# The opening of a hybrid decoder trunk: modulation sums moved from VectorE to TensorE's column groups, and six product tiles instead of four

## The chip, the cores and the metric

One core of a Trainium2 chip runs the whole kernel in one launch. The metric is the device time of one execution in microseconds, the median of the runs shown. A profile is one execution recorded by the hardware profiler.

## The reference

Two layers; each is a SwiGLU feed-forward half-step, a mixing step (windowed attention, an RWKV-7 recurrence and a short convolution side by side) and a second SwiGLU half-step. Every sub-layer begins with an RMS norm whose result is scaled and shifted by columns that come from the conditioning vector `c`. The part around the change, cut to what matters:

```python
c_act = jax.nn.silu(c)                                   # (1, 1024)
for l in range(2):
    mod = (c_act @ w_ada[l] + b_ada[l]).reshape(1, 9, 1024)
    sh1, sc1, gt1, sh2, sc2, gt2, sh3, sc3, gt3 = ...     # nine rows of 1024
    hn = rms_norm(h, g_ffn1[l]) * (1.0 + sc1) + sh1       # h: (512 tokens, 1024)
    h = h + 0.5 * (1.0 + gt1) * swiglu(hn, w_ffn1_in[l], w_ffn1_out[l])
    ...                                                   # mixing and second SwiGLU, in the same manner
def swiglu(x, w_in, w_out):
    gate, up = jnp.split(x @ w_in, 2, axis=-1)            # 1024 -> 2 x 2816
    return (jax.nn.silu(gate) * up) @ w_out
```

## The kernel before

The residual lies transposed in SBUF: eight tiles `h[k]` of 128 features by 512 tokens (`T`, `KD` = 8). A float32 product is made of three TensorE matmuls in the format fp32r: both operands are split into a rounded part H and the rest L, and `mm3` adds wH·xH, wH·xL and wL·xH. A weight tile is split by `split`: ScalarE writes H, then VectorE writes L = source - H. One output tile (128 x 512) takes 8 x 3 = 24 matmuls of 512 columns and fills one bank of PSUM. PSUM has eight banks in four tags of two (`mm`, `r0`, `r1`, `x`).

The tile framework puts the instructions of each engine in a fixed order when the kernel is built, by the order of the program, its priorities and a model of when each is ready; `tc.issue_after(x)` and `tc.add_manual_dep` pin an instruction behind another on the same engine. Each engine then runs its list in order. SP issues the weight loads (`nc.sync.dma_start`), POOL (`nc.gpsimd.dma_start`) those of the later modulation weights.

`begin` (L1143 to L1255) is the opening. It makes the modulation of the first norm (rows sc1 and sh1 of layer 0, each 8 blocks of 128 columns) and the first four output tiles of the first SwiGLU's input product. Its modulation weights come in four groups `m` of two blocks each, in tiles of 1 MB. `scales(m)` and `shifts(m)` compute three of a group's four columns with `ada_dot` (L190), one VectorE instruction over 1024 elements that multiplies by a replicated silu(c) (`crep`, made by TensorE and ScalarE at L1200 to L1205) and sums along the row; the fourth column is made of eight TensorE matmuls with one moving column (L1180). `normed(k)` then makes block k of the normed activations: z = h·rstd on VectorE, reading rstd from PSUM; scale and shift on ScalarE (L1187); H on ScalarE, L on VectorE. `warm(n)` issues n matmuls whose result nobody reads. The groups of products go over n (output tile) and k (block): after the second product of group m, the modulation and norm of group m+1 are placed.

The pool `first` (L1257) holds the opening's modulation weights, raw weight tiles and small columns. When `begin` returns, the pool is closed and `ffn` (L337) opens its own pool in its place. `ffn` receives the finished PSUM tiles as `first`; `projector` (L292) goes on from there with the weights of tile 4 and later, up to tile 15, each loaded by SP into `wraw` (two buffers) and split into `wH` and `wL` (four buffers each in the pool `wp`). At the same time `ada_crep` (L194) loads c again into the new pool and `ada_steps` (L200) lets POOL load the next modulation columns, three buffers at a time, and VectorE sum them, in steps of 0, 0, 4, 4, 0, 3, 0, 0 behind the pairs of output tiles. After tile 15, `pair_in` makes the rest of the input product in another form (seven half-size products a pair).

Of the kernel before, what the change touches and what calls it, by code (L numbers as in the profile page):

```python
# [8 lines left out]
F32 = mybir.dt.float32  # L9
# [23 lines left out]
GAP = 448  # L33
GROUPS = ((0, 12), (12, 22))
# [24 lines left out]
def trunk_kernel(ctx, tc, ins, out, layers=L, phases=("ffn1", "mix", "ffn2")):  # L59
# [57 lines left out]
    def mm3(acc, w, k, x, sl, start, stop):  # L117
# [5 lines left out]
        mm(acc, wL, xH, start=False, stop=stop)  # L123
# [1019 lines left out]
    def begin(pool):  # L1143
# [3 lines left out]
        col = {n: pool.tile([P, KD], F32, name=n, tag=n) for n in ("sc", "sh", "gb", "gm0", "sh0")}  # L1147
        stt(col["gb"], bsc, 1.0, g1, ALU.add, ALU.mult)
        wa, wf, ws = {}, [], []

        def fetch(m):
            for n in (0, 2):
                w = pool.tile([P, 2, D], F32, name="wada", tag="wada", bufs=8)
                nc.sync.dma_start(w, ins["wa0"][m, :, n : n + 2])
                wa[m, n], wa[m, n + 1] = w[:, 0], w[:, 1]

        def fetch_w():
            j, g = divmod(len(wf), 2)
            w = pool.tile([P, KD, P], F32, name="wfirst", tag="wfirst", bufs=4)
            nc.sync.dma_start(w, ins["w1i"][0, j, g])  # L1160
            wf.append(w)

        def split_w(n):
            pair = tuple(wp.tile([P, KD, P], F32R, name=x, tag=x, bufs=4) for x in ("wH", "wL"))
            split(*pair, wf[n])
            ws.append(pair)

        def scales(m):
            for n in range(2):
                k = slice(2 * m + n, 2 * m + n + 1)  # L1170
                ada_dot(col["sc"][:, k], wa[m, n], crep)
                stt(col["gm0"][:, k], col["sc"][:, k], g1[:, k], col["gb"][:, k], ALU.mult, ALU.add)

        def shifts(m):
            k0, k1 = (slice(2 * m + n, 2 * m + n + 1) for n in range(2))
            ada_dot(col["sh"][:, k0], wa[m, 2], crep)
            tt(col["sh0"][:, k0], col["sh"][:, k0], bsh[:, k0], ALU.add)
            pt = psum([P, 1], "ps_ada")
            for k in range(KD):
                mm(pt, wa[m, 3][:, k * P : (k + 1) * P], cact[:, k : k + 1], start=k == 0, stop=k == KD - 1)  # L1180
            tt(col["sh0"][:, k1], pt, bsh[:, k1], ALU.add)

        def normed(k):
            z = E("z")
            tt(z, h[k], rstd, ALU.mult)
            x = E("hn_t")
# [184 lines left out]
```

## Time and profile before

| | |
|---|---|
| time, median of 3 runs | 1867.47 us (1863.78 to 1871.30) |
| profiled execution | 1866.04 us, span 1864.0 us |
| granted TensorE clock over the span | 0.994 |
| busy: PE, DVE, ACT, POOL | 1828.7, 1398.4, 836.3, 130.9 us |
| TensorE idle before the first product of the opening, and within it | 2.87 us, 1.56 us |
| read from HBM, mean rate | 302.66 MB, 164 GB/s |

Times in the rows are microseconds from the start of the span. PE is TensorE's matmul, PEld its weight load, DVE VectorE, ACT ScalarE, POOL GpSimd, SP the engine that issues DMAs. A timeline row has start, duration, engine, line, operation, output<-inputs, tile shape, count, and in brackets the engine's idle time before it and what ended that. A row of the groups has busy time, mean ns of one, idle time before and what ended it. Matmuls overlap in the pipeline: their spacing is read from start to start. An fp32 matmul shows as two instructions, an fp32r one as one.

### The profile page before, as it was taken

Reading aid. Unit: us, or ns where it says so; the run is one execution under the profiler, and the core shown is the slowest. Engines: PE = TensorE matmul, PEld = TensorE weight load, DVE = VectorE, ACT = ScalarE, POOL = GpSimd, SP = SyncE. Lnnn points to the kernel's source line nnn. Section 1 sums busy time; section 2 is a strip of 40 time slices with the busy share of each in tenths; the row PEclk is TensorE's granted clock in tenths of the full one; section 3 lists DMA queues with packets and bytes.
Section 4 is the critical chain, followed back from the end, with each engine's and each line's share of the span. In section 5 each row is a group of like instructions: output and inputs, shape, how many; then the busy total and the mean of one; then the engine's idle time right before and its main releaser. Section 6 shows DMA issues by size and latency. Waiting matters only on the chain.

```text
span 1864.0 us, 33421 instructions
## 1 busy us (share of the span) xinstructions
PE 1828.7 (98%) x13664; PEld 1644.4 (88%) x13664; DVE 1398.4 (75%) x2202; ACT 836.3 (45%) x1272; POOL 130.9 (7%) x212
## 2 busy tenths in 40 slices
PE   8999999999999999999999999999999999999999
PEld 6889899986777999899999988999767788998998
DVE  7687677867986887777878786777589778874872
ACT  4443255346422555245345524544563335532551
POOL 0101110100000000110100020110000000100100
PEclk8999999999999999999999999999999999999999
DMA  7667876621122475886737688773212125775752
GB/s 307 225 185 234 263 197 202 221 83 46 58 55 72 136 195 176 296 223 195 246 112 197 171 272 228 192 229 114 101 56 59 53 68 161 209 227 139 203 144 68
DMA packets 104313, 308.24 MB, mean 165 GB/s; under 512 B 23392, under 2 KB 24416, under 8 KB 103136
## 3 DMA queue, kind: packets, MB, share of 16 engines
q1 hardware_dynamic: 75936, 203.34, 32.3%
q0 software_dynamic: 28224, 102.77, 21.7%
q8 instruction: 107, 1.75, 0.4%
q14 instruction: 46, 0.38, 0.1%
HBM read 302.66 MB, written 3.41 MB: 164 GB/s over the span
## 4 chain that ended last, share of the span: by engine, by line
PE 71%; DVE 13%; DMA 7%; issue 4%; ACT 4%; POOL 1%; SPq 0%; POOLq 0%; DVEq 0%; ACTq 0%
PE ps_mm L121 11%; PE ps_mm L122 10%; PE ps_mm L123 10%; PE ps_d L420 6%; PE ps_d L422 6%; PE ps_d L421 6%; PE ps_f L420 3%; PE ps_f L422 3%; PE ps_f L421 3%; DMA wada<-in_wadaT 2%; DVE wL L135 2%; PE ps_g L422 2%; PE ps_g L420 2%; PE ps_g L421 2%; ACT wH L133 1%
## 5 line engine op out<-in xcount | busy, mean ns | idle before, releaser
L133 ACT CAST wH<-wraw 128x1024 fp32r<-128x1024 f32 (+2 forms) x292 | 266.1, 918 | 434.7 <-PE ps_mm L122 190.2
L135 DVE TENSOR_TENSOR wL<-wraw,wH 128x1024 fp32r<-128x1024 f32 (+2 forms) x292 | 307.2, 1058 | 105.1 <-ACT wH L133 104.4
L123 PE MATMUL ps_mm<-actH,wL 128*128 128x512 f32 (+1 forms) x784 | 281.5, 359 | 2.8 <-DVE wL L135 2.8
L121 PE MATMUL ps_mm<-actH,wH 128*128 128x512 f32 (+1 forms) x784 | 281.6, 359 | 0.0
L122 PE MATMUL ps_mm<-actL,wH 128*128 128x512 f32 (+1 forms) x784 | 281.2, 359 | 0.0
L121 PE MATMUL ps_mm<-hnH,wH 128*128 128x512 f32 (+1 forms) x760 | 267.5, 359 | 5.7 <-ACT hnH L133 2.9
L122 PE MATMUL ps_mm<-hnL,wH 128*128 128x512 f32 (+1 forms) x760 | 266.5, 353 | 0.5
L123 PE MATMUL ps_mm<-hnH,wL 128*128 128x512 f32 (+1 forms) x760 | 266.4, 353 | 0.6 <-DVE wL L135 0.6
L420 PE MATMUL ps_d<-comH,wH 128*128 128x256 f32 x816 | 224.7, 275 | 0.3 <-ACT s L446 0.3
L421 PE MATMUL ps_d<-comL,wH 128*128 128x256 f32 x816 | 224.4, 275 | 0.0
L422 PE MATMUL ps_d<-comH,wL 128*128 128x256 f32 x816 | 224.4, 275 | 0.0
L192 DVE SCALAR_TENSOR_TENSOR wada<-wada,crep 128x1024 f32<-128x1024 f32 x140 | 167.7, 1219 | 48.8 <-DMA wada<-in_wadaT 48.2
L135 DVE TENSOR_TENSOR wL<-sum,wH 128x1024 fp32r<-128x1024 f32 x102 | 124.9, 1224 | 71.5 <-ACT wH L133 71.3
L123 PEld LDWEIGHTS ps_mm<-actH,wL 128*128 128x128 f32 x784 | 149.1, 190 | 20.3 <-DVE wL L135 3.6
L121 PEld LDWEIGHTS ps_mm<-hnH,wH 128*128 128x128 f32 x760 | 143.4, 191 | 24.9 <-issue 3.8
L121 PEld LDWEIGHTS ps_mm<-actH,wH 128*128 128x128 f32 x784 | 149.1, 190 | 16.8
L122 PEld LDWEIGHTS ps_mm<-actL,wH 128*128 128x128 f32 x784 | 149.0, 190 | 16.8
L123 PEld LDWEIGHTS ps_mm<-hnH,wL 128*128 128x128 f32 x760 | 145.5, 191 | 19.3 <-issue 4.3
L122 PEld LDWEIGHTS ps_mm<-hnL,wH 128*128 128x128 f32 x760 | 145.4, 192 | 17.2 <-DVE hnL L277 1.6
L420 PEld LDWEIGHTS ps_d<-comH,wH 128*128 128x128 f32 x816 | 156.7, 192 | 0.9 <-ACT s L446 0.9
L422 PEld LDWEIGHTS ps_d<-comH,wL 128*128 128x128 f32 x816 | 156.7, 192 | 0.0
L421 PEld LDWEIGHTS ps_d<-comL,wH 128*128 128x128 f32 x816 | 156.7, 192 | 0.0
(354 smaller groups left out, 3855.6 us busy)
## 6 DMA issues: line engine op xcount, KB each, us to landing
wada<-in_wadaT POOLq DMA_DIRECT2D x128, 512.0 KB, 4.8
wraw<-in_wmi SPq DMA_DIRECT2D x40, 512.0 KB
wraw<-in_w2p SPq DMA_DIRECT2D x36, 512.0 KB
wraw<-in_w1p SPq DMA_DIRECT2D x32, 512.0 KB
wraw<-in_w1o SPq DMA_DIRECT2D x32, 384.0 KB
wraw<-in_w2o SPq DMA_DIRECT2D x32, 384.0 KB
wraw<-in_w1i SPq DMA_DIRECT2D x20, 512.0 KB
wraw<-in_w1o SPq DMA_DIRECT2D x32, 320.0 KB
```

What stands on the lines that cost most here:

```text
L121: mm(acc, wH, xH, start=start, stop=False)
L122: mm(acc, wH, xL, start=False, stop=False)
L123: mm(acc, wL, xH, start=False, stop=stop)
L133: nc.scalar.copy(hi, src)
L135: return nc.vector.tensor_sub(lo, src, hi.bitcast(F32))
L192: stt(w, w, 1.0, crep, ALU.mult, ALU.mult, accum_out=out_)
L420: mm(acc, wH, xH, start=start and i + k == 0, stop=False, skip_group_check=True)
L421: mm(acc, wH, xL, start=False, stop=False, skip_group_check=True)
L422: mm(acc, wL, xH, start=False, stop=k == 3, skip_group_check=True)
```

## The change

- The modulation weights of one block k, its scale and shift columns side by side (1024 rows by 256 columns, 1 MB), are one tile. `modulation(k)` streams them through TensorE: the stationary operand is a 32-column tile of `cz` whose first column is silu(c) and whose others are zero; the eight 128-row slices go in turn to four column groups of 32, so that four partial rows stand in PSUM. ScalarE copies the 128 x 256 result to `part`, two small matmuls with ones sum it into a scale column and a shift column, and VectorE makes `gm0` and `sh0` from them. The eight matmuls have high priority and are pinned behind each other and behind the product given as `behind`.
- `crep`, `scales` and `shifts` are gone from the opening.
- `normed` writes z = h·gm0·rstd in one VectorE instruction, with rstd copied to SBUF, H directly on ScalarE from z and the shift, L in one VectorE instruction; one ScalarE pass less for each block.
- Six output tiles are begun in the opening, not four. `begin` writes out the order of products, modulations, norms and weight splits by hand. Weights 4 and 5 are split into buffers of the pool `first`.
- The loads follow the list `WANTED`, one modulation tile and one weight tile in turn at first.
- A ScalarE instruction with Sqrt stands ahead of the squares. `warm` stands at other places, and its bank is of tag `x`.

```diff
--- before.py
+++ after.py
@@ -31,6 +31,7 @@
 BASE = 16
 PAD = 24
 GAP = 448
+WANTED = (0, 1, 0, 1, 0, 1, 0, 1, 0, 0, 1, 0, 1, 0)
 GROUPS = ((0, 12), (12, 22))
 RWKV_WORK, ATT_WORK, FILL_WORK = 29.8, 15.2, 129.6
 
@@ -120,7 +121,7 @@
         acc = paired(acc)
         mm(acc, wH, xH, start=start, stop=False)
         mm(acc, wH, xL, start=False, stop=False)
-        mm(acc, wL, xH, start=False, stop=stop)
+        return mm(acc, wL, xH, start=False, stop=stop)
 
     latest = {}
 
@@ -1144,114 +1145,131 @@
         hn = [tuple(hnp[k // 4].tile([P, T], F32R, name=n, tag="hn") for n in ("hnH", "hnL")) for k in range(KD)]
         g1 = prm(0, "g1")
         bsh, bsc = (prm(0, "b_ada")[:, i * KD : (i + 1) * KD] for i in range(2))
-        col = {n: pool.tile([P, KD], F32, name=n, tag=n) for n in ("sc", "sh", "gb", "gm0", "sh0")}
-        stt(col["gb"], bsc, 1.0, g1, ALU.add, ALU.mult)
-        wa, wf, ws = {}, [], []
-
-        def fetch(m):
-            for n in (0, 2):
-                w = pool.tile([P, 2, D], F32, name="wada", tag="wada", bufs=8)
-                nc.sync.dma_start(w, ins["wa0"][m, :, n : n + 2])
-                wa[m, n], wa[m, n + 1] = w[:, 0], w[:, 1]
+        col = {n: pool.tile([P, KD], F32, name=n, tag=n) for n in ("gb", "gm0", "sh0")}
+        wa, wf, ws = [], [], []
+
+        def fetch():
+            w = pool.tile([P, KD, 2 * P], F32, name="wada", tag="wada", bufs=6)
+            nc.sync.dma_start(w, ins["wa0"][len(wa)])
+            wa.append(w)
 
         def fetch_w():
             j, g = divmod(len(wf), 2)
-            w = pool.tile([P, KD, P], F32, name="wfirst", tag="wfirst", bufs=4)
+            w = pool.tile([P, KD, P], F32, name="wfirst", tag="wfirst", bufs=6)
             nc.sync.dma_start(w, ins["w1i"][0, j, g])
             wf.append(w)
 
         def split_w(n):
-            pair = tuple(wp.tile([P, KD, P], F32R, name=x, tag=x, bufs=4) for x in ("wH", "wL"))
-            split(*pair, wf[n])
+            home, bufs = (wp, 4) if n < 4 else (pool, 2)
+            pair = tuple(home.tile([P, KD, P], F32R, name=x, tag=x, bufs=bufs) for x in ("wH", "wL"))
+            split(*pair, wf[n], ("part", "row") if n else None)
             ws.append(pair)
 
-        def scales(m):
-            for n in range(2):
-                k = slice(2 * m + n, 2 * m + n + 1)
-                ada_dot(col["sc"][:, k], wa[m, n], crep)
-                stt(col["gm0"][:, k], col["sc"][:, k], g1[:, k], col["gb"][:, k], ALU.mult, ALU.add)
-
-        def shifts(m):
-            k0, k1 = (slice(2 * m + n, 2 * m + n + 1) for n in range(2))
-            ada_dot(col["sh"][:, k0], wa[m, 2], crep)
-            tt(col["sh0"][:, k0], col["sh"][:, k0], bsh[:, k0], ALU.add)
-            pt = psum([P, 1], "ps_ada")
-            for k in range(KD):
-                mm(pt, wa[m, 3][:, k * P : (k + 1) * P], cact[:, k : k + 1], start=k == 0, stop=k == KD - 1)
-            tt(col["sh0"][:, k1], pt, bsh[:, k1], ALU.add)
-
-        def normed(k):
-            z = E("z")
-            tt(z, h[k], rstd, ALU.mult)
-            x = E("hn_t")
-            act(x, z, AF.Identity, bias=col["sh0"][:, k : k + 1], scale=col["gm0"][:, k : k + 1])
-            split(*hn[k], x)
-
-        pw = psum([P, T], "ps_warm", "r1")
+        pw = psum([P, T], "ps_warm")
         wide = ones_r.unsqueeze(1).to_broadcast([P, 4, P])
 
-        def warm(n):
-
-            for _ in range(n):
-                mm(pw.rearrange("p (a b) -> p a b", b=P), ones_r, wide, start=True, stop=True)
+        def warm(n, behind=None):
+
+            with tc.issue_after(behind.ins) if behind else nullcontext():
+                for _ in range(n):
+                    mm(pw.rearrange("p (a b) -> p a b", b=P), ones_r, wide, start=True, stop=True)
 
         warm(3)
-
-        crep = pool.tile([P, D], F32, name="crep", tag="crep")
-        for hf in range(2):
-            pt = psum([P, 4, P], "ps_crep")
-            for k in range(4):
-                mm(pt[:, k], cT[:, 4 * hf + k : 4 * hf + k + 1].to_broadcast([P, P]), cst("ident"), start=True, stop=True)
-            act(crep[:, hf * 512 : hf * 512 + 512], pt.rearrange("p k n -> p (k n)"), AF.Silu)
-        fetch(0)
-        fetch_w()
-        fetch_w()
-        fetch(1)
-        fetch_w()
-        fetch_w()
-        fetch(2)
-        fetch(3)
+        cz = pool.tile([P, KD, CH // 2], F32, name="cz", tag="cz")
+        nc.gpsimd.memset(cz, 0.0)
+        nc.vector.tensor_copy(cz[:, :, 0], cact)
+        act(col["sh0"][:, :1], cact[:, :1], AF.Sqrt, bias=vals["eps"], scale=0.0)
+        for w in WANTED:
+            (fetch, fetch_w)[w]()
         nc.sync.dma_start(con[:, P:], ins["con"][:, P:])
-        warm(20)
+        warm(22)
+        stt(col["gb"], bsc, 1.0, g1, ALU.add, ALU.mult)
         ss = new_ss()
         for i in range(KD):
             add_ss(ss, i)
-
         pt = psum([P, NB], "ps_ss")
         for b in range(NB):
-            mm(pt[:, b : b + 1], ss[:, b * P : (b + 1) * P], ones[:, :1], start=True, stop=True)
-        warm(3)
+            m = mm(pt[:, b : b + 1], ss[:, b * P : (b + 1) * P], ones[:, :1], start=True, stop=True)
+        warm(3, m)
         r = pool.tile([P, NB], F32, name="rstd_t", tag="rstd_t")
         act(r, pt, AF.Sqrt, bias=vals["eps"], scale=1.0 / D)
         nc.vector.reciprocal(r, r)
-        rstd = psum([P, T], "ps_rstd", "r0")
+        pt = psum([P, T], "ps_rstd")
         for b in range(NB):
-            mm(rstd[:, b * P : (b + 1) * P], r[:, b : b + 1].to_broadcast([P, P]), cst("ident"), start=True, stop=True)
-        warm(2)
-        scales(0)
-        shifts(0)
-        warm(8)
+            mm(pt[:, b * P : (b + 1) * P], r[:, b : b + 1].to_broadcast([P, P]), cst("ident"), start=True, stop=True)
+        rstd = pool.tile([P, T], F32, name="rstd", tag="rstd")
+        nc.scalar.copy(rstd, pt)
+
+        def modulation(k, rest=0, behind=None):
+
+            pt = psum([P, 2 * P], "ps_ada")
+            with tc.high_priority():
+                for i in range(KD):
+                    j = slice(i % 4 * 32, i % 4 * 32 + 32)
+                    m = mm(pt[j], cz[:, i], wa[k][:, i], start=i < 4, stop=i >= 4)
+                    if behind is not None:
+                        tc.add_manual_dep(m.ins, behind.ins.name, ORDER, reason="column groups run together")
+                    behind = m
+            part = pool.tile([P, 2 * P], F32, name="part", tag="part", bufs=2)
+            latest["part"] = nc.scalar.copy(part, pt)
+            ada = m
+            warm(rest // 2, m)
+            pt = psum([P, 2], "ps_col")
+            for i in range(2):
+                last = mm(pt[:, i : i + 1], part[:, i * P : (i + 1) * P], ones[:, :1], start=True, stop=True)
+            warm(rest, last if rest else None)
+            c = slice(k, k + 1)
+            stt(col["gm0"][:, c], pt[:, :1], g1[:, c], col["gb"][:, c], ALU.mult, ALU.add)
+            tt(col["sh0"][:, c], pt[:, 1:], bsh[:, c], ALU.add)
+            return ada
+
+        def normed(k):
+            z, sh = E("hn_t"), col["sh0"][:, k : k + 1]
+            latest["row"] = stt(z, h[k], col["gm0"][:, k : k + 1], rstd, ALU.mult, ALU.mult)
+            act(hn[k][0], z, AF.Identity, bias=sh)
+            stt(hn[k][1], z, sh, hn[k][0].bitcast(F32), ALU.add, ALU.subtract)
+
+        pts = [psum([P, T], "ps_mm", tag) for tag in ("r0", "r1", "mm") * 2]
+
+        def go(*jobs):
+            for n, k in jobs:
+                last = mm3(pts[n], ws[n], k, hn[k], ALL, k == 0, k == KD - 1)
+            return last
+
+        split_w(0)
+        modulation(0, 4)
+        second = modulation(1)
         normed(0)
-        split_w(0)
+        with tc.issue_after(second.ins):
+            last = go((0, 0))
+        normed(1)
         split_w(1)
-        normed(1)
-        pts = [psum([P, T], "ps_mm", tag) for tag in ("mm", "mm", "r1", "r0")]
-        for m in range(4):
-            groups = [(n, 2 * m + k) for k in range(2) for n in range(4)]
-            if m == 0:
-                groups = [(n, k) for n0 in (0, 2) for k in range(2) for n in (n0, n0 + 1)]
-            elif m == 3:
-                groups = [(n, 6 + k) for n in range(4) for k in range(2)]
-            for g, (n, k) in enumerate(groups):
-                mm3(pts[n], ws[n], k, hn[k], ALL, k == 0, k == KD - 1)
-                if m < 3 and g == 1:
-                    scales(m + 1)
-                    shifts(m + 1)
-                    if m == 0:
-                        split_w(2)
-                        split_w(3)
-                    normed(2 * m + 2)
-                    normed(2 * m + 3)
+        last = go((1, 0))
+        modulation(2, 2, last)
+        last = go((0, 1), (1, 1))
+        normed(2)
+        split_w(2)
+        last = go((2, 0), (2, 1))
+        modulation(3, 2, last)
+        go((0, 2), (1, 2), (2, 2))
+        normed(3)
+        split_w(3)
+        last = go((3, 0), (3, 1))
+        modulation(4, 0, last)
+        normed(4)
+        last = go((3, 2), (0, 3), (1, 3), (2, 3))
+        modulation(5, 0, last)
+        normed(5)
+        split_w(4)
+        last = go((3, 3), *((n, 4) for n in range(4)))
+        modulation(6, 0, last)
+        normed(6)
+        last = go(*((4, k) for k in range(5)))
+        split_w(5)
+        modulation(7, 0, last)
+        normed(7)
+        go(*((n, 5) for n in range(5)), *((5, k) for k in range(6)))
+        go(*((n, 6) for n in range(6)), *((n, 7) for n in range(6)))
         return hn, pts
 
     with tc.tile_pool(name="first", bufs=1) as fp:
@@ -1298,8 +1316,8 @@
 
     wT = i["w_ada"].reshape(L, D, 9, KD, P).transpose(0, 2, 3, 4, 1)
     a["wadaT"] = c(wT)
-    last = i["w_ada"][0, :, :D].reshape(KD, P, 4, 2, P)[:, :, :, 1].transpose(2, 1, 0, 3).reshape(4, P, D)
-    a["wa0"] = c(np.stack([wT[0, 1, ::2], wT[0, 1, 1::2], wT[0, 0, ::2], last], axis=2))
+    first = i["w_ada"][0].reshape(KD, P, 9, KD, P)[:, :, 1::-1]
+    a["wa0"] = c(first.transpose(3, 1, 0, 2, 4).reshape(KD, P, KD, 2 * P))
     a["crep"] = c(np.broadcast_to(i["c"].reshape(1, D), (P, D)))
     for n, w in (("w1", "w_ffn1_in"), ("w2", "w_ffn2_in")):
         a[n + "i"] = c(i[w].reshape(L, KD, P, 2, NF, P)[:, :, :, :, :8].transpose(0, 4, 3, 2, 1, 5))
```

## The prediction

> **What bounds the kernel now.** I read the page first: the kernel as a whole is a TensorE stream.
>
> ```profile
> span 1864.0 us, 33421 instructions
> PE 1828.7 (98%) x13664; PEld 1644.4 (88%) x13664; DVE 1398.4 (75%) x2202; ACT 836.3 (45%) x1272; POOL 130.9 (7%) x212
> ```
>
> The execution took 1866.04 us, 2.0 more than its span; the median of the three runs, 1867.47, is 1.4 above it. Only the opening is edited, so I then read that stretch: stage windows, TensorE's timeline, the groups of instructions, the queues.
>
> ```profile
> 10.00:20.00 10.00, 7.99 (x51) 6.82 (x49) 7.62 (x18) 3.67 (x6) 0.00 (x0) 0.97 1.02 425
> 20.00:30.00 10.00, 7.70 (x30) 5.87 (x30) 9.38 (x17) 5.66 (x8) 0.00 (x0) 0.67 1.01 415
> 30.00:40.00 10.00, 9.46 (x36) 7.99 (x37) 7.15 (x13) 2.34 (x4) 0.00 (x0) 0.68 0.88 356
> 40.00:50.00 10.00, 9.77 (x55) 8.21 (x55) 7.53 (x18) 5.02 (x8) 0.52 (x1) 1.00 0.00 0
> ...
> 16.41 1.84 PE L1180 MATMUL ps_ada<-cact,wada 128*128 128x1 f32 x16
> 21.12 0.79 PE L121 MATMUL ps_mm<-hnH,wH 128*128 128x512 f32 x1 [2.87 <-ACT hnH L133]
> 30.54 0.79 PE L121 MATMUL ps_mm<-hnH,wH 128*128 128x512 f32 x1 [1.56 <-ACT wH L133]
> 55.39 0.38 PE L123 MATMUL ps_mm<-hnH,wL 128*128 128x512 f32 x1
> 65.75 0.38 PE L123 MATMUL ps_mm<-hnH,wL 128*128 128x512 f32 x1
> ```
>
> The window columns are time, then busy time of PE, PEld, DVE, ACT, POOL, granted clock, DMA share, GB/s. From 20 to 30 us VectorE is the full engine (9.38 of 10), TensorE waits (2.87 us before its first product, 1.56 at 30.54), and its clock is 0.67. The first product matmul starts at 21.12; the 96th (four tiles) at 55.39, the 144th (the two tiles after them) at 65.75. These 48 are (65.75-55.39)/48 = 0.216 us apart, the full rate. So 144 products need 31.1 us, the 144th ends its slot at 65.97, and 65.97-21.12-31.1 = 13.8 us of the opening are lost to waits, half clock and modulation matmuls. The changed opening holds the same 144 products, so I compare the time at which the 144th is through; what follows is common to both.
>
> **The change part by part.** Removed from VectorE: the twelve 1024-wide sums.
>
> ```profile
> L192 DVE SCALAR_TENSOR_TENSOR wada<-wada,crep 128x1024 f32<-128x1024 f32 x12 | 14.3, 1217 | 0.0
> L1185 DVE TENSOR_TENSOR z<-h,ps_rstd 128x512 f32<-128x512 f32 x8 | 5.5, 681 | 0.3 <-ACT hn_t L1187 0.3
> L135 DVE TENSOR_TENSOR wL<-wfirst,wH 128x1024 fp32r<-128x1024 f32 x4 | 4.9, 1222 | 1.4 <-ACT wH L133 1.3
> L1205 ACT ACTIVATE crep<-ps_crep 128x512 f32<-128x512 f32 x2 | 1.2, 594 | 0.7 <-PE ps_crep L1204 0.7
> L1187 ACT ACTIVATE hn_t<-z,sh,gm 128x512 f32<-128x512 f32 x8 | 6.4, 811 | 20.6 <-DVE sh L1177 20.5
> L133 ACT CAST wH<-wfirst 128x1024 fp32r<-128x1024 f32 x4 | 4.1, 1037 | 1.1 <-DMA wfirst<-in_w1i 1.1
> ```
>
> 14.3 us of VectorE go. It keeps per block z and hnL (0.68 each) and two one-column steps; six weight splits of 1.22 make 7.3. Some 21 us over a 40 us stretch no longer fill it. ScalarE loses one cast per block and the two crep passes, and gains a copy of each product row; it had 5.66 of 10 at most. Neither bounds the opening any more. The sqrt table load moves ahead of the squares: covered by the loads of h; without that cover it costs its 1.3 us. The one memset on POOL lies in its idle time.
>
> Added to TensorE per block: eight fp32 matmuls of 256 moving columns in four 32-column groups, then two one-column sums. The nearest rows are the attention product, fp32, 512 columns, in two 64-column groups.
>
> ```profile
> 446.22 1.08 PE L1059 MATMUL ps_av<-pmc,V 128*64 128x512 f32 x4
> 447.13 1.03 PE L1059 MATMUL ps_av<-pmp,V 128*64 128x512 f32 x4
> 448.09 1.13 PE L610 MATMUL ps_kk<-kksq,con 128*128 128x512 f32 x2
> ```
>
> An fp32 matmul shows as two instructions. One pair of groups takes 447.13-446.22 = 0.91 us, while a single full-array one (L610) is about as long, 1.1: two groups run together. Half the columns make 0.455 per round; four groups together need two rounds, 0.91, and the two pairs above took 448.09-446.22 = 1.87, or 0.05 more than 1.82. I add 0.16 for entering and leaving the mode: 1.07 per block. Bounds: 0.9, and 8 x 0.455+0.16 = 3.8 if nothing overlaps; I take 1.07 because the row is the same kind of instruction. The two sums are four instructions of the L1180 kind (1.84/16 = 0.115): 0.46.
>
> The Trainium skill, TensorEngine Tiling (Array Packing), Key Properties, says that changing the tiling mode drains TensorE, which speaks against eight such excursions; the rows above bound that at a few tenths each. Its page TensorE: Matmul & The Clock Gate, Part 3, measured 3.07x for four row tiles, not 4x; by that, as an estimate, a block costs 3.64/3.07+0.16 = 1.35, and the forecast would rise by 1.7 us.
>
> The loads: wa tiles stay 1 MB each, now one per block with a weight tile behind it, all on SP.
>
> ```profile
> 13.17 5.38 SPq L1154 DMA_DIRECT2D wada<-in_wa  x4
> ...
> SPq L1154 <- DMA wada<-in_wa: 4.2, 2, 2.2
> ```
>
> The issue at 13.17 was released by the landing of an earlier wada, the first: so block 0 is there at about 13.2. At 0.42 MB/us (the 425 and 415 GB/s above) 1.05 MB takes 2.5 us, a weight tile 1.25. Block 1 lands at 16.9, weight tile 1 at 18.2, block 2 at 20.7, weight tile 2 at 21.9, block 7 at 38.2. Bytes and issues ahead of the next stage (two more weight tiles, two fewer wraw) are about equal; the issues of blocks 6 and 7 wait on SP for buffers that blocks 0 and 1 free long before; the constants and wraw behind them are not needed until later.
>
> First product after the change:
>
> ```profile
> 11.92 0.69 DVE L235 TENSOR_TENSOR ss<-ss,sq 128x512 f32<-128x512 f32 x1
> 12.67 1.05 PE L1222 MATMUL ps_ss<-ones_r,ss 128*128 128x1 f32 x8 [0.26 <-DVE ss L235]
> 13.76 0.26 ACT L1225 ACTIVATE rstd_t<-ps_ss,v_eps 128x4 f32<-128x4 f32 x1 [1.50 <-PE ps_ss L1222]
> 15.52 1.05 PE L1229 MATMUL ps_rstd<-con,rstd_t 128*128 128x128 f32 x8
> ```
>
> The sum of squares ended at 12.6; without the two crep passes (0.6 each) between the squares I take 11.6. Then ps_ss 1.05, sqrt and reciprocal 0.5, ps_rstd 1.05, its new copy 0.6: 14.9. ps_warm now holds one of the two "x" banks, so block 0's modulation follows that copy: 1.07, copy of its row 0.4 (half the columns of the 0.594 copy, and a start), sums 0.46, the two column steps 0.4, z 0.68, hnH 0.81: 18.7, with hand-overs 19.0, against 21.12. Block 1's modulation lies inside this. Bounds 17.5 (block 0 ahead of ps_rstd) and 20.5.
>
> From there: products 31.1; blocks 2 to 7, 6 x 1.07 = 6.4; sums 7 x 0.46 = 3.2; six warm matmuls after blocks 2 and 3, 6 x 0.216 = 1.3; waits: tile 1 needs its weight tile (18.2), wH (1.04) and wL (1.22), 1.3 us; the sums wait for the row's copy, filled mostly by products or warm matmuls, 0.1 each, 0.7 (bounds 0 and 3). Sum 19.0+31.1+6.4+3.2+1.3+1.3+0.7 = 63.0, against 65.97: **3.0 us earlier**. Blocks 3 to 7 are in long before their turn (block 7 at 38.2 for a turn near 46). 1866.0-3.0 = 1863.0 for an execution like the profiled one, 1864.4 on the scale of the median. That is the forecast.
>
> **Rivals.** *A half-clock spell remains.*
>
> ```profile
> 16.01:19.42 3.41, 2.24 (x21) 2.15 (x20) 3.29 (x10) 0.62 (x1) 0.00 (x0) 1.00 1.04 430
> 19.42:26.25 6.83, 4.98 (x11) 3.60 (x12) 5.67 (x7) 4.98 (x7) 0.00 (x0) 0.50 1.02 417
> 26.25:29.66 3.41, 2.73 (x21) 2.27 (x19) 3.37 (x11) 0.93 (x2) 0.00 (x0) 1.00 1.01 413
> 43.31:46.72 3.41, 3.29 (x21) 2.70 (x19) 3.41 (x8) 0.12 (x1) 0.00 (x0) 1.00 0.00 0
> ```
>
> The spell at 0.50 follows a window in which TensorE was 2.24 of 3.41 us busy, much of it one-column matmuls; after 2.73 the clock fell again; after 3.29, with as many such matmuls, it did not. In the new order the stretch from 16 to 23 us has some 0.7 of streaming, nearer the last. A spell of 6.83 us costs 3.4: 1867.8. The skill's clock page (TensorE: Matmul & The Clock Gate, Part 1) throttles after an idle window of about 3.4 us; by that there would be no spell here and the forecast stands, but the two rows do not bear a wholly idle window out.
>
> *VectorE piles up behind the opening (slower).*
>
> ```profile
> 49.19 0.33 SPq L196 DMA_DIRECT2D crep<-in_crep  x1
> SPq L196 <- ACT hn_t L1187: 12.5, 1, 12.5
> 54.71 1.06 ACT L197 ACTIVATE crep<-crep 128x1024 f32<-128x1024 f32 x1
> 69.55 1.22 DVE L192 SCALAR_TENSOR_TENSOR wada<-wada,crep 128x1024 f32<-128x1024 f32 x1
> 72.99 2.36 DVE L135 TENSOR_TENSOR wL<-wraw,wH 128x1024 fp32r<-128x1024 f32 x2
> ```
>
> The load of the next stage's crep waited for the last reader of the opening's pool. Two weight pairs now lie in that pool, so the last reader is the last product (63.0): crep is ready 54.71+1.06-49.19 = 6.6 us later. Then come three sums (69.55 to 72.99), to 63.0+10.0, and in the profile two weight splits stood behind such a group. If the split of tile 7, needed 5.6 us after the opening, stands there too, it is done at 11.3 and TensorE waits 5.7, with a spell 9.1: 1870.1 to 1873.5. It decides if VectorE's order puts that split behind the sums; against it, its bytes are there before crep.
>
> *Column groups run one after another:* 6 x (3.8-1.07) = 16.4 and one more block ahead of the first product, 2.7: 1883.5. The L1059 rows speak against it.
>
> *More is won:* first product at 17.5 and no waits, 3.5 us, and later stalls dissolve with the new phase.
>
> ```profile
> PE ps_mm L123 <- DVE wL L135: 2.4, 1, 2.4
> PE ps_g L422 <- DVE wL L135: 1.1, 1, 1.1
> PE ps_g L420 <- ACT wH L133: 1.0, 1, 1.0
> ```
>
> These are all the waits from 66 to 230 us: 4.5, and 1.7 of half clock behind the longest. All of it gives 1854.7.
>
> **How the numbers follow.** Forecast 0.42; half-clock spell 0.18; VectorE pile-up 0.15; groups in sequence 0.05; more won 0.20. About 0.5%, 9.3 us, is what a measurement of this kernel can tell from no change: below 1858.1 lies two thirds of the last case (0.13); above 1876.8 the serial groups and a fifth of the pile-up with more stalls behind it (0.08); the rest, 0.79, between. The range 1857 to 1873 leaves out half of the gains' tail (0.10), the serial groups (0.05) and the pile-up's upper end (0.03). The forecast's own range, by the bounds of the first product and the waits, is 1862 to 1868.
>
> **What would show it.** Right: eight groups of 16 ps_ada matmuls of about 1.1 us each; the first product near 19; a granted clock of 1.0 from 20 to 50; the 144th product through near 63; no VectorE group above 8 of 10 before it. Wrong: ps_ada groups of 2 us or more; a clock of 0.5 inside the products; a TensorE wait on wL within 12 us after the opening; or the opening gaining its 3 us while the waits after 66 us grow by as much.

## The result, and the profile after

The changed kernel is slower: 1878.15 us median (1871.6 to 1885.81, 20 runs) against 1868.02 us (1861.48 to 1877.23, 20 runs) for the kernel before, a ratio of 1.0062 [1.0048, 1.0076]. Some 10 us are lost where 3 were to be won. The profiled execution took 1883.28 us; its page, span, engines and clock row:

```profile
span 1881.4 us, 33589 instructions
PE 1839.2 (98%) x13748; PEld 1647.2 (88%) x13748; DVE 1387.3 (74%) x2179; ACT 833.6 (44%) x1272; POOL 131.5 (7%) x213
PEclk9999999999999999999999999999999999999999
```

VectorE does 11 us less than before, and TensorE is busy 10.5 us longer. The stage windows of the changed kernel (time, PE, PEld, DVE, ACT, POOL busy, clock, DMA share, GB/s) answer to the four of before:

```profile
10.00:20.00 10.00, 7.06 (x44) 5.51 (x44) 2.62 (x7) 3.27 (x6) 0.00 (x0) 0.83 1.02 421
20.00:30.00 10.00, 8.18 (x52) 4.11 (x51) 5.35 (x8) 3.65 (x6) 0.00 (x0) 0.84 1.02 416
30.00:40.00 10.00, 9.37 (x62) 6.56 (x64) 5.61 (x10) 3.19 (x5) 0.00 (x0) 0.99 1.01 413
40.00:50.00 10.00, 10.00 (x84) 6.96 (x77) 4.56 (x9) 3.32 (x6) 0.00 (x0) 1.00 0.13 53
```

VectorE fell from 9.38 of 10 to 5.35 and is no longer near full; the clock at 20 to 30 us rose from 0.67 to 0.84. The first came as forecast, the second in part (a clock of 1.0 was foretold), and TensorE is still no earlier. Its timeline:

```profile
12.44 1.21 PE L1192 MATMUL ps_ss<-ones_r,ss 128*128 128x1 f32 x8 [2.22 <-DVE ss L236]
14.94 1.85 PE L1199 MATMUL ps_rstd<-con,rstd_t 128*128 128x128 f32 x8
17.51 1.07 PE L1209 MATMUL ps_ada<-wada,cz 128*32 128x256 f32 x16 [0.72 <-issue]
21.64 0.48 PE L122 MATMUL ps_mm<-hnH,wH 128*128 128x512 f32 x1
27.06 1.93 PE L1209 MATMUL ps_ada<-wada,cz 128*32 128x256 f32 x16
69.73 0.38 PE L124 MATMUL ps_mm<-hnH,wL 128*128 128x512 f32 x1
69.95 0.38 PE L122 MATMUL ps_mm<-hnH,wH 128*128 128x512 f32 x1
```

The first product starts at 21.64 (before 21.12), and the slot of the 144th ends at 69.95 (before 65.97): the opening is 4.0 us later, not 3.0 earlier. A block's column groups take 1.07 us, as priced; the 1.93 and the 1.85 for `ps_rstd` (1.05 before) lie in stretches at half clock. These stretches, and one later, each behind the window ahead of it:

```profile
9.78:13.19 3.41, 1.19 (x9) 0.77 (x8) 2.37 (x5) 1.32 (x3) 0.00 (x0) 1.00 1.01 414
13.19:16.60 3.41, 3.41 (x14) 3.07 (x13) 0.18 (x1) 0.27 (x1) 0.00 (x0) 0.50 1.01 424
23.42:26.84 3.42, 2.11 (x9) 1.06 (x8) 2.80 (x5) 0.72 (x1) 0.00 (x0) 1.00 1.02 412
26.84:30.25 3.41, 3.41 (x20) 1.73 (x20) 0.00 (x0) 1.14 (x2) 0.00 (x0) 0.50 0.99 408
125.83:129.24 3.41, 0.07 (x1) 0.07 (x1) 1.32 (x2) 1.37 (x2) 0.00 (x0) 1.00 0.56 166
129.24:136.07 6.83, 6.32 (x28) 5.96 (x28) 6.26 (x7) 4.47 (x6) 0.86 (x1) 0.50 0.59 163
```

The second loss follows the opening. VectorE's and the queues' rows of the changed kernel, then those of the kernel before:

```profile
70.18 0.33 SPq L197 DMA_DIRECT2D crep<-in_crep  x1
70.76 1.77 POOL L207 DMA_DIRECT2D wada<-in_wadaT  x3 [69.70 <-DVE silu L504]
77.18 1.23 DVE L193 SCALAR_TENSOR_TENSOR wada<-wada,crep 128x1024 f32<-128x1024 f32 x1 [1.49 <-ACT crep L198]
102.64 4.90 DVE L389 TENSOR_TENSOR x<-hnH,hnL 128x512 f32<-128x512 f32 x8
124.51 0.33 SPq L369 DMA_DIRECT2D first<-in_w1p  x1
128.07 1.04 ACT L134 CAST wH<-first 128x1024 fp32r<-128x1024 f32 x1 [1.91 <-DMA first<-in_w1p]
129.17 0.54 PE L421 MATMUL ps_d<-hnH,wH 128*128 128x256 f32 x1 [4.58 <-ACT wH L134]
```

```profile
49.48 1.77 POOL L206 DMA_DIRECT2D wada<-in_wadaT  x3 [49.02 <-ACT hn_t L1187]
93.13 4.90 DVE L388 TENSOR_TENSOR x<-hnH,hnL 128x512 f32<-128x512 f32 x8
115.02 0.33 SPq L368 DMA_DIRECT2D first<-in_w1p  x1
120.44 0.28 PE L420 MATMUL ps_d<-hnH,wH 128*128 128x256 f32 x1
```

The opening's pool now closes behind the last product, so both queues' first loads into the next pool, crep on SP and the modulation columns (wada) on POOL, come 21 us later than before (70.18 for 49.19, 70.76 for 49.48), and the first sum on VectorE 7.6 us later (77.18 for 69.55). (POOL's row names a silu of VectorE that ended at about the same time; in e1, below, where the pool closes earlier, this load came at 63.83, released by a product.) VectorE works through a fixed list, and at L389 it is 9.5 us late (102.64 for 93.13), while TensorE was 4.0 late. Not all of it is a wait for crep: VectorE stood only 1.49 us for it, and ahead of that it had the silu and L steps of the tiles that end together behind the opening. The weights of the first half-size product wait for VectorE, their load is also 9.5 us late (124.51 for 115.02), and TensorE stands for 4.58 us; 6.83 us at half clock follow.

To the end of the pairs stage (the first full-size product behind the half-size ones) this makes 97.95 us from the slot's end, 92.32 before. So the profiled pair of kernels differs by 4.0 us at the opening's end, 5.6 more in the pairs stage (2.9 of waits, up to 3.4 for half clock) and 7.6 in the rest (up to 3.4 for half clock, 3.5 of waits): 17.2 of the spans' 17.4 us. The medians differ by only 10.1: part of the rest is this execution's own.

### The profile page after: what moved, and what is told of

The parts are those of the page before. It is cut to its first block, busy times and chain, and to the rows that moved or that the text cites. A ratio compares the mean times of both kernels' runs of the same rounds, so it can differ in the third digit from the quotient of the medians.

```text
span 1881.4 us, 33589 instructions
## 1 busy us (share of the span) xinstructions
PE 1839.2 (98%) x13748; PEld 1647.2 (88%) x13748; DVE 1387.3 (74%) x2179; ACT 833.6 (44%) x1272; POOL 131.5 (7%) x213
## 3 DMA queue, kind: packets, MB, share of 16 engines
q0 software_dynamic: 28224, 102.77, 21.5%
q8 instruction: 108, 1.77, 0.4%
HBM read 302.66 MB, written 3.41 MB: 163 GB/s over the span
## 4 chain that ended last, share of the span: by engine, by line
PE 66%; DVE 13%; DMA 10%; issue 6%; ACT 3%; POOL 1%; SPq 0%; DVEq 0%; POOLq 0%; ACTq 0%
PE ps_mm L122 9%; PE ps_mm L123 9%; PE ps_mm L124 9%; PE ps_d L421 6%; PE ps_d L422 6%; PE ps_d L423 6%; DMA wada<-in_wadaT 4%; PE ps_f L422 3%; PE ps_f L423 3%; PE ps_f L421 3%; DVE wL L136 2%; PE ps_g L423 2%; PE ps_g L422 1%; PE ps_g L421 1%; ACT wH L134 1%
## 5 line engine op out<-in xcount | busy, mean ns | idle before, releaser
L193 DVE SCALAR_TENSOR_TENSOR wada<-wada,crep 128x1024 f32<-128x1024 f32 x128 | 154.0, 1221 | 57.1 <-DMA wada<-in_wadaT 55.3
L123 PEld LDWEIGHTS ps_mm<-hnL,wH 128*128 128x128 f32 x760 | 144.3, 190 | 17.4 <-issue 1.8
```

The costliest lines, as they stand in the source:

```text
L123: mm(acc, wH, xL, start=False, stop=False)
L193: stt(w, w, 1.0, crep, ALU.mult, ALU.mult, accum_out=out_)
```

## The experiments

Half clock comes in stretches of 3.41 us or multiples and differs from one execution of a kernel to the next (the mean granted clock of the changed kernel's 20 runs lies between 0.990 and 0.997), so each profile is read by the same marks. The first is the start of the first product, the next the end of the 144 products' time (the start of the 145th), then the distance from there to the end of the pairs stage (the first full-size product behind them; the last two expectations call that mark the first half-size product), then from there to the end of the last TensorE matmul. In brackets: us at half clock, then us that TensorE waited.

| kernel | first product | 144 through (half clock so far) | pairs stage (half, waits) | rest (half, waits) |
|---|---|---|---|---|
| before | 21.12 | 65.97 (13.7) | 92.3 (0, 2.2) | 1701.9 (6.8, 21.7) |
| after | 21.64 | 69.95 (6.8) | 98.0 (6.8, 5.1) | 1709.4 (13.7, 25.3) |
| e1_order | 21.45 | 68.20 (3.4) | 95.1 (0, 4.5) | 1701.4 (3.4, 22.3) |
| e2_four | 25.59 | 72.57 (13.7) | 94.9 (3.4, 2.9) | 1697.9 (3.4, 19.7) |
| e3_before6 | 22.13 | 66.05 (13.7) | 98.9 (6.8, 6.2) | 1705.6 (6.8, 24.3) |
| e4_warm | 19.83 | 66.58 (0) | 96.6 (3.4, 5.1) | 1705.1 (6.8, 25.2) |
| e5_double | 22.73 | 73.22 (0) | 98.4 (6.8, 6.2) | 1700.2 (3.4, 22.1) |
| e6_half_sums | 21.35 | 68.31 (13.7) | 91.8 (0, 2.0) | 1700.2 (3.4, 21.5) |
| e7_clock | 22.43 | 64.30 (0) | 91.9 (0, 2.1) | 1700.8 (3.4, 21.3) |
| e8_warm_order | 20.28 | 67.04 (0) | 94.4 (0, 3.8) | 1709.7 (10.2, 27.7) |
| e9_four_warm | 20.23 | 71.23 (10.2) | 95.4 (3.4, 3.5) | 1702.5 (6.8, 22.6) |
| e10_six_clock | 24.59 | 64.25 (3.4) | 97.7 (6.8, 5.2) | 1705.1 (6.8, 24.3) |

The rest, less half of its half clock and less its waits, is 1676.4 to 1677.9 us in all twelve. So, to within 1.5 us, nothing but waits and half clock sets one kernel's rest apart from another's.

**e1_order: the pool closes earlier.** The last twelve product groups of the changed opening are put in an order in which the tiles of the pool's weights come first:

```diff
-        go(*((n, 6) for n in range(6)), *((n, 7) for n in range(6)))
+        go(*((n, k) for k in (6, 7) for n in (4, 5)), *((n, k) for n in range(4) for k in (6, 7)))
```

> Edit: only the order of the opening's last twelve products: tiles 4 and 5 take blocks 6 and 7 first, then tiles 0 to 3. Theory (pool): the load of the next stage's crep and its modulation columns waits for the last reader of the opening's pool, which since the change is the last product (SP's row: crep issued at 70.18); here that reader ends 8 products, 5.2 us, earlier, so crep is issued near 65, VectorE's first sum starts near 72 instead of 77.2, and TensorE's wait at the first half-size products (4.6 us at 129.2) falls below 2 us; the time falls by 3 to 6 us against the changed kernel, to about 1872 to 1875. Rival (bunching): VectorE is late because the steps of three pairs and the splits of tiles 6 and 7 all come right behind the opening; then crep comes earlier but the wait stays at 4 to 5 us and the time at about 1878.

1875.26 us, 1.0039 [1.0021, 1.0058]. Crep was issued at 63.26, 4.9 us ahead of the slot's end; the wait on wH at the first half-size product is gone, and the pairs stage is 95.1. Two of its rows, and the longest waits of TensorE from 100 to 235 us:

```profile
63.26 0.33 SPq L197 DMA_DIRECT2D crep<-in_crep  x1
97.41 4.90 DVE L389 TENSOR_TENSOR x<-hnH,hnL 128x512 f32<-128x512 f32 x8
```

```profile
PE ps_f L423 <- DVE wL L136: 1.6, 1, 1.6
PE ps_g L423 <- DVE wL L136: 1.0, 1, 1.0
PE ps_g L421 <- ACT wH L134: 1.0, 1, 1.0
```

The pool is a cause, but not the only one: the ratio stays above 1. VectorE reaches L389 29.2 us behind the slot's end (97.41-68.20), where the changed kernel took 32.7 and the kernel before 27.2: the earlier pool takes away 3.5 us of VectorE's 5.5 us delay, and 2.0 stay, which may be the rival's bunching. By the times alone the two kernels are hardly apart (the intervals of their ratios overlap); e8 repeats the step on e4.

**e2_four: column groups alone, with the rest of the change (norm, loads, order).** `WANTED` ends after the fourth weight tile, and tiles 4 and 5 go back to `projector`:

```diff
-WANTED = (0, 1, 0, 1, 0, 1, 0, 1, 0, 0, 1, 0, 1, 0)
+WANTED = (0, 1, 0, 1, 0, 1, 0, 1, 0, 0, 0, 0)
-        pts = [psum([P, T], "ps_mm", tag) for tag in ("r0", "r1", "mm") * 2]
+        pts = [psum([P, T], "ps_mm", tag) for tag in ("mm", "mm", "r1", "r0")]
...
```

> Edit: the changed opening with four product tiles instead of six; the modulation still streams through TensorE, nothing of the weights lies in the opening's pool. Both theories of the wait after the opening (pool and bunching) expect it back at about 2 us. Theory that the modulation on TensorE is what costs: the 144th product is still through only near 69 to 70 (before: 66.0, changed: 69.95) and the time stays near 1874. Rival, that six tiles cost it: the 144th product is through at 66 to 67 and the time is that of before, 1868.

1875.42 us, 1.0038 [1.0020, 1.0056]. In the profile 13.65 us at half clock lay between 12.09 and 25.75, nearly all ahead of the first product, so the 72.57 can't settle whether TensorE's own work made the opening late, and the time is near the theory's 1874. Four tiles had no wait on wH at the first half-size product.

**e3_before6: six tiles alone.** The kernel before with weights 4 and 5 in the opening's pool and six tiles begun:

```diff
-            pair = tuple(wp.tile([P, KD, P], F32R, name=x, tag=x, bufs=4) for x in ("wH", "wL"))
+            home, bufs = (wp, 4) if n < 4 else (pool, 2)
+            pair = tuple(home.tile([P, KD, P], F32R, name=x, tag=x, bufs=bufs) for x in ("wH", "wL"))
...
+            elif m == 2:
+                split_w(4)
+                groups += [(4, k) for k in range(6)]
...
```

> Edit: the kernel before, with its sums on VectorE, but six product tiles begun in the opening, weights 4 and 5 in the opening's pool and rstd copied to SBUF (the bank is needed). If six tiles delay the next stage: crep is issued only with the last product, TensorE's wait at the first half-size products is 4 us or more (before: 2.1 us in two pieces), and the time is 3 to 6 us above before, about 1872 to 1874. If the new modulation is what delays it: the wait stays near 2 us and the time at 1868 or below, as more products cover the opening's waits.

1870.99 us, 1.0025 [1.0010, 1.0041]. The opening ends where it did (66.05 for 65.97), but crep was issued at 66.24 and the half-size products paid. Two of its TensorE waits, from 100 to 235 us:

```profile
PE ps_d L420 <- ACT wH L133: 5.7, 1, 5.7
PE ps_mm L123 <- DVE wL L135: 2.5, 1, 2.5
```

With e2 this splits the result: six tiles +0.25%, column groups +0.38%, both +0.62%.

**e4_warm: the changed kernel at a kept clock in the opening.** Eleven more unread matmuls ahead of the sum of squares:

```diff
-        warm(22)
+        warm(33)
```

> Edit: 33 instead of 22 unread matmuls ahead of the sum of squares, which fill the 2.2 us in which TensorE was idle from 10.2 to 12.4. Theory: the half-clock spell from 13.2 to 16.6 follows that idle stretch; without it ps_rstd takes 1.05 instead of 1.85 us, the first product starts near 20.6 instead of 21.6 and the 144th is through 1 us earlier; the time falls by about 1 us, too little to be told. Rival: the spell comes anyway (the sums of squares have one column only) and the first product stays at 21.6.

1877.42 us, 1.0054 [1.0035, 1.0072]. The clock stayed at 1.0 through the whole opening, and the 144 products were through at 66.58, 3.4 us earlier (1 was expected; the second stretch went too): still not ahead of the kernel before, which had 13.7 us at half clock. The changed opening's own work is what takes the time. Its groups of TensorE instructions from 10 to 74 us (busy us, mean ns of one), then the one of the kernel before:

```profile
L1209 PE MATMUL ps_ada<-wada,cz 128*32 128x256 f32 x128 | 8.6, 385 | 0.7 <-issue 0.7
L1219 PE MATMUL ps_col<-ones_r,part 128*128 128x1 f32 x32 | 4.1, 232 | 0.0
```

```profile
L1180 PE MATMUL ps_ada<-cact,wada 128*128 128x1 f32 x64 | 7.4, 245 | 0.0
```

**e5_double: is TensorE the bound of the new opening?** On e4, each block's eight modulation matmuls are issued twice:

```diff
-                for i in range(KD):
+                for i in (*range(KD), *range(KD)):
                     j = slice(i % 4 * 32, i % 4 * 32 + 32)
```

> Edit: e4_warm with every block's eight column-group matmuls issued twice (the second pass starts over, the result is the same). Theory: in the changed opening TensorE itself is the bound from the first product on, so six more passes of 1.0 us behind the first product, and the first two ahead of it, move the 144th product by 7 to 8 us, from 66.4 to about 73.5 to 74.5. Rival: the passes lie in waits for VectorE, ScalarE and the loads; then it moves by less than 3 us.

1877.77 us (one run). The 144 products were through at 73.22, 6.6 us behind e4 (7 to 8 were expected), with no half clock in either: 2.9 us ahead of the first product and 3.7 between the products, where the column groups took 5.2 us more. TensorE's waits there fell only from 2.46 to 1.36 us. So TensorE is the bound of the new opening: most of what it is given comes out. The end of that execution doesn't show it, because its rest was 4.9 us shorter by waits and half clock.

**e6_half_sums: was VectorE the bound of the old opening?** In the kernel before, each of the twelve sums runs over 512 columns:

```diff
-                ada_dot(col["sc"][:, k], wa[m, n], crep)
+                ada_dot(col["sc"][:, k], wa[m, n][:, :512], crep[:, :512])
...
-            ada_dot(col["sh"][:, k0], wa[m, 2], crep)
+            ada_dot(col["sh"][:, k0], wa[m, 2][:, :512], crep[:, :512])
```

> Edit: the kernel before with each of the opening's twelve VectorE sums over 512 columns instead of 1024 (the other half of each modulation sum is left out). Saves 7 us of VectorE. Theory, that VectorE's sums were not what the opening lost most to: the first product starts 1.2 to 2 us earlier, the 144th is through 2 to 4 us earlier, near 62 to 64, and half-clock spells remain. Rival, the reading in the prediction, that VectorE bounds the opening: the 144th is through 7 us earlier or more, near 59.

1866.41 us (one run); 144 products through at 68.31, later than before, where the theory had 62 to 64 and the rival 59. Its window from 20 to 30 us, then a row of VectorE's and one of TensorE's timeline:

```profile
20.00:30.00 10.00, 7.31 (x28) 5.80 (x28) 7.01 (x16) 3.96 (x6) 0.00 (x0) 0.66 1.01 413
```

```profile
29.25 0.16 DVE L1181 TENSOR_TENSOR sh<-ps_ada,par 128x1 f32<-128x1 f32 x1 [2.18 <-PE ps_ada L1180]
27.37 1.84 PE L1180 MATMUL ps_ada<-cact,wada 128*128 128x1 f32 x16
```

VectorE is down to 7.01 of 10, and now stands idle 2.18 us for the shift column that TensorE makes. The clock is as low as before (0.66), and TensorE's waits within the products rose from 1.95 to 3.95 us, most of them for ScalarE's hnH and wH. In this execution half of the sums gone bought nothing; what it would buy at a kept clock was not run.

**e7_clock: the kernel before at a kept clock.** Unread matmuls, pinned behind the one-column ones:

```diff
-        warm(20)
+        warm(29)
-        warm(3)
+        warm(8, m)
-        shifts(0)
-        warm(8)
+        warm(12, shifts(0))
...
+                    if m == 0:
+                        warm(14, behind)
```

> Edit: the kernel before with unread matmuls pinned behind the modulation matmuls of groups 0 (12) and 1 (14) and more of them ahead of and behind the sum of squares (29 and 8), so that TensorE streams through its two waits. Theory, that half clock cost before some 6 us of its opening (12 us of spells among its products): the granted clock stays at 1.0 from 12 to 50 us, the 144th product is through near 61 to 63 instead of 66.0, and the time is 3 to 5 us below before, about 1863. Rival: at full clock TensorE only waits longer for VectorE's sums; the 144th is through at 64 to 66 and the time is that of before.

1863.38 us (1857.81 to 1866.08, 12 runs), 0.9984 [0.9971, 0.9998]: the one version that beats both. Its window where before had a clock of 0.67:

```profile
20.00:30.00 10.00, 9.48 (x47) 7.15 (x46) 8.72 (x18) 5.63 (x8) 0.00 (x0) 1.00 1.02 416
```

With VectorE's sums all in place, 144 products were through at 64.30. The time is the theory's, the 64.30 is the rival's (64 to 66). So part of the time before was lost by the clock, but of the up to 6.0 us that half clock cost among its products only 1.7 came back at the end of the 144: 14 unread matmuls now stand between them, 14 x 0.216 = 3.0 us, and without these TensorE might have waited for VectorE's sums at full clock. No run takes that apart.

**e8_warm_order: e4 and e1 together.**

```diff
-        warm(22)
+        warm(33)
-        go(*((n, 6) for n in range(6)), *((n, 7) for n in range(6)))
+        go(*((n, k) for k in (6, 7) for n in (4, 5)), *((n, k) for n in range(4) for k in (6, 7)))
```

> Edit: e1_order and e4_warm together, the changed kernel with both of its losses mended that are known. Theory: the 144th product is through near 66.4 as in e4_warm, the waits and spells after the opening are as in e1_order (95.4 us from the 144th to the 385th product), so the 385th starts near 161.8, 3.5 us behind before, and the time is 2 to 5 us above before, about 1870 to 1872: even mended, the change gains nothing. Rival: the two mends make up the whole 10 us and the time is that of before or less, 1866 to 1868.

1873.49 us, 1.0029 [1.0011, 1.0047]. Both remedies work in the profile (67.04 with no half clock, pairs stage 94.4 for e4's 96.6), and the kernel is still slower than the one before, and than the 1870 to 1872 expected.

**e9_four_warm and e10_six_clock: the two halves again, at a kept clock.** The first is e2 with `warm(33)`, the second e3 with e7's unread matmuls:

```diff
-        warm(22)
+        warm(33)
```

```diff
-        shifts(0)
-        warm(8)
+        warm(12, shifts(0))
...
```

> The changed kernel with four product tiles (weights 4 and 5 not in the opening's pool), and warm(33) in place of warm(22), so that the clock stays at 1.0. It is the column groups alone, at a kept clock; its partners are the kernel before with its clock kept (1863.4 us, 144th product through at 64.3) and the changed kernel with its clock kept (1877.4 us, 66.6). Theory (TensorE is the bound of the changed opening: about 10 us of modulation, column and warm matmuls and hand-overs where before had 5): the 144th product starts its slot at 66 to 67, the first half-size product 94 to 95 us later (160 to 162), time 1868 to 1872. Rival (the column groups lost only by half-clock spells): 144th at 64 to 65, time 1863 to 1866. Rival (the pool of the opening is what costs, and four tiles free it early): as the kernel before with its clock kept after the opening, 92 to 93 us from the 144th to the first half-size product.

> The kernel before with six product tiles (weights 4 and 5 split into buffers of the opening's pool) and the unread matmuls that kept the clock of the kernel before at 1.0. It is the six tiles alone at a kept clock. Theory (two weights in the opening's pool hold back the load of crep until the last product; VectorE runs its fixed order late and TensorE meets it where the half-size products begin): the 144th product at 64 to 65, the first half-size product 97 to 100 us later, with one wait of 4 to 6 us on ACT wH or the like, time 1867 to 1871. Rival (the six tiles lost by spells alone): 144th at 64, distance 92 to 93, time 1862 to 1865.

e9: 1873.66 us, 1.0031 [1.0015, 1.0048]. The clock was not kept, and neither the 66 to 67 of its theory nor the 1868 to 1872 came: 10.24 us at half clock lay inside its products. Without the 5.1 us which that costs at most the 71.23 would be 66.1, near e4's 66.58; by its profile alone this run can't tell the column groups' price from that of the spell. e10: 1871.25 us, 1.0023 [1.0006, 1.0040]. No half clock inside the products, 144 through at 64.25 as in e7, and then 97.7 us where e7 had 91.9, with the waits

```profile
PE ps_d L420 <- ACT wH L133: 4.5, 1, 4.5
PE ps_d L420 <- ACT s L446: 3.2, 1, 3.2
```

So six tiles cost 1871.25-1863.38 = 7.9 us at a kept clock, 7.3 by the ratios, each of which is taken against the kernel before in the same round. In their profiles 5.8 us of difference lie in the pairs stage. A wait of 3.4 to 5.7 us on wH stands at the first half-size product in all five six-tile kernels whose pool closes behind the last product (after, e3, e4, e5, e10); in the others it is 0.6 us or less.

## Why the prediction was wrong, point by point

**The steps that failed.** There are two, of about the same size. One is the opening's own sum, 63.0 for a measured 69.95: 2.6 in the first product, 2.8 behind it at full clock (nearly all a term left out), 1.6 in a spell. The other is "what follows is common to both": the pairs stage took 5.6 us longer in the profiled execution, and if that execution's opening is typical, some 6 of the 10.1 us between the medians lie behind it.

**What bounds the kernel.** The prediction read VectorE at 9.38 of 10 as the engine that holds TensorE up from 20 to 30 us. VectorE was full, but its sums were not what the time hung on alone: e6 took half of each away, and with the clock as low as before the opening was no earlier; e7 left them in, kept the clock, and was faster. Of the 44.85 us from the first product to the end of the 144, TensorE waited only 1.95, and 11.96 lay at half clock, which costs up to 6.0. So the relief of VectorE had little to give at that clock, and the work that went to TensorE had to be paid. What the relief is worth at a kept clock stays open.

**The sum for TensorE.** Given 31.1 for the products, the old opening spent 5.11 us on `ps_ada` between them. The new one at full clock (e4) spent 6.0 on the column groups (predicted 6.4), 2.54 on the column sums (3.2), 1.77 on unread matmuls (1.3), and 2.46 on waits (2.0 together): 43.9 of the 44.0 foretold. It took 46.75. The 2.9 us between are the term left out. They lie in slots of products that are longer than 0.216 us: 1.5 of them beside modulation and column matmuls, some 0.1 us at each change from one kind to the other, and 1.4 mostly beside TensorE's waits. In the profiled execution the spell at 26.84 added 1.6: 48.3.

**Column groups run together: right.** They take 1.07 us per block at full clock. The rule of the Trainium skill, TensorE: Matmul & The Clock Gate, Part 3 (3.07x for four row tiles), would make it 1.35; the trace, with its 1.07, does not agree with it for these column groups. The draining that TensorEngine Tiling (Array Packing), Key Properties, tells of agrees in kind with the 1.5 us at the changes; no run took it apart from the other causes of a hand-over.

**First product at 19.0: wrong.** It came at 21.64. Without half clock (e4) it was 19.83, inside the bounds. The sum of squares ended at 12.4, not 11.6, which makes 0.8 of the 2.6: taking the crep passes away brought it forward by only 0.2 from before's 12.6. From there to the first product it took 9.2 us, in e4 at full clock 7.8, in the prediction 7.4 (its first terms make 14.8, not 14.9): so the spell at 13.19 cost 1.4, and 0.4 are the chain's own.

**The clock.** Fewer stretches at half clock, as hoped (3.4 us inside the products for 12.0), yet not none. The rival that gave a spell 3.4 us was right in kind. The stretch at 26.84 followed a window in which TensorE was 2.11 of 3.41 us busy. The Trainium skill, TensorE: Matmul & The Clock Gate, Part 1, asks for an idle window; the trace agrees for the stretch at 129.24, whose window had 0.07 us busy, and does not for the two early ones, since neither window ahead of them was idle (1.19 and 2.11 us busy).

**VectorE behind the opening: the rival that was right.** Its mechanism held in the main: pool, crep after the last product, sums late; e1 shows that some 2 of VectorE's 5.5 us behind TensorE come from something else. Its price was foreseen at the split of tile 7, 11.3 us after the opening. VectorE had slack there, and the price fell 59 us later, where the half-size stage leaves it none (10.00 of 10 busy from 110 to 120). Of POOL's loads of wada, late by the same 21 us, the prediction said nothing. The first sums now wait for their loads (up to 1.48 us, ahead of the one at 91.41), and VectorE's delay grows from 7.6 to 9.5 us.

**Cases that were ruled out rightly or fell.** Column groups in sequence: refuted by the 1.07. More is won: no run of the changed kernel shows it. The chance of 0.08 for slower by over 0.5% was too small because the pile-up and the spell, each added to an opening 3.0 us earlier, were taken as alternatives: 1870.1 to 1873.5 for the first, 1867.8 for the second. The opening was 4.0 later instead, and the losses add up. The pile-up's price itself, 5.7 us or 9.1 with a spell, was near the mark, and in all five kernels with the wait of 3.4 to 5.7 us half clock followed it.

**What stays open.** The profiles give the column groups some 2 us in the opening (66.6 for e7's 64.3) and 2.5 to 3.5 in the pairs stage (e8 and e9, 94.4 and 95.4, for e7's 91.9), of which in e9 up to 1.7 are a stretch at half clock. The medians give them 7 (1.0038). What is left lies in the rest, which varies by up to 12 us from profile to profile, and one profile a kernel can't share it out. That the six-tile kernels wait 1.8 to 3.8 us near 1000 us where the others wait 0 to 1.2 was seen in every profile, and its cause was not tried.

## What to carry to other kernels

A full engine beside a waiting one is not yet the bound: read what the waiting engine's own time is made of (clock, waits, its own instructions) before work is moved onto it. If work is moved to the engine that sets the end, it must be paid there instruction by instruction, here with about 0.1 us for each change between kinds of matmul. Here a buffer in a pool held back what the next pool loads: ask which instruction reads the pool last, list every queue that waits for it, and follow the delay to the next place where the late engine has no slack.

## What the runs showed of the hardware

Half clock came in stretches of 3.41 us or multiples, and they differed between executions of the same stage (the changed kernel and e1 are alike until the last products; one had stretches at 13.19 and 26.84, the other one at 13.47). Over the twelve profiles the full-clock window ahead of a stretch had from 0 to 2.94 us of its 3.41 busy, and others with as little as 1.5 were followed by full clock. So no busy time of one window parts the two, and a single profile can't price a wait. Four column groups of 32, fp32, with 256 moving columns, ran side by side: eight matmuls, from the first's start at 18.83 to the product behind them at 19.83 in e4, took 1.00 us.
